# First block of a two-block model: attention's queries and keys ahead of the forget gates, and the gated recurrence in the last, skewed output projection

## The chip, the cores and the metric

The kernel runs on one core of one Trainium2 chip. The metric is the time of one launch in device microseconds (us). Before the change it is 1415.68 us, the median of three runs.

## What is computed

Two blocks of two layers each work on a sequence of 256 tokens of width 1024, in float32. The change touches the two layers of the first block. Each of them normalises the tokens, multiplies them with a wide input matrix, and runs three branches of width 512 on the columns of the product: causal attention with eight heads of 64 (queries and keys normalised by head and turned by a position-dependent rotation), a gated linear recurrence with four heads of 128 (HGRN), and attention over 256 rows of a memory with four heads of 128. Each branch is multiplied by silu of its own gate columns, and the three together by an output matrix:

```python
for l in range(DEPTH):
    h = rms_norm(x, norm_g[l])
    q_a, k_a, v_a, q_h, f_h, i_h, q_m, z = jnp.split(h @ w_in[l], split_points, axis=-1)
    o_a = moba_attention(qa, ka, va)                      # branch 0
    o_h = rms_norm(hgrn2_chunkwise(q_h, f_h, i_h, lb_all[l]), hgrn_o_norm[l])   # branch 1
    o_m = memory_attention(qm, km, vm)                    # branch 2
    y = jnp.concatenate([o_a, o_h, o_m], axis=-1) * jax.nn.silu(z)
    x = x + y @ w_out[l]
```

The second block (a delta rule, a retention and a pooling branch, then a gated feed-forward) follows and is not touched.

## The kernel before

The tokens lie in two tiles of 128 (t is 0 or 1). Every weight matrix is streamed once from memory in units of 256 rows x 512 columns. `Stream` keeps a list of the units in the order of their use (`units1` for this block, line 859 and on). A unit is loaded by SP into one of five `raw` buffers, ScalarE rounds it to a high half (`wh`), and VectorE makes the low half (`wl`, the difference), after which the raw buffer is free for the load five units later. A weight product is then three matmuls (high by high, high by low, low by high), which `mm3` issues at line 137; `aTh` and `aTl` are the two halves of the turned activations. Results lie in three PSUM banks named `acc` and five named `mx`.

`layer1` (line 920 and on) writes one layer. `tok` gives products with tokens as rows, `chan` with channels as rows (for `f_h` and `q_h` of the recurrence), `out_proj` the output projection. Everything that is not a weight product is a generator that is handed to `Order.spawn`. `Order` is a planner: it keeps modelled times of the engines, and after each group of three matmuls `poll` lets every waiting generator go one step whose inputs it believes to be ready. So weight products are the filler, and the branches' small steps stand between them in TensorE's order. A scheduler of the layer below may still shift instructions. The order of each engine is fixed when the program is built; a waiting instruction holds up all behind it on its engine.

Names that matter: `hgrn_f` makes the forget gates' sums `hA` and the gated keys `hk`; `hgrn` runs once for each of two pairs of heads, in eight levels of lengths 256, 128, ... 2 (`hgrn_z`: VectorE `hE`, ScalarE exponentials, VectorE `hZ`, then a product of `hZ` with itself on TensorE) and a last one of `hq` and `hk`; results of the five shortest levels are merged into `hST` by `COPY_PREDICATED` on VectorE. `hgrn_out` multiplies `hST` (and `hS01` of the earlier chunk) by `i_sb`, and normalises by head: a square (`junk`) on ScalarE, a sum (`ss`) on VectorE, logarithm and exponential on ScalarE (`y`), small steps, `on`. `gated` multiplies `on` by `sz`, turns the product `y` (transposes on TensorE) and splits it into `aTh` (ScalarE) and `aTl` (VectorE). `moba_in` and `moba` are the attention, `mem_attn` the attention over memory.

The order in a layer is: `i_h`, `v_a`, `f_h`, `q_h`, `q_a`, `k_a`, in layer 0 the memory's keys and values of both layers (16 units), `q_m`, and the gates `z` of branches 1, 0, 2. Then `out_proj` for branch 1 without skew, and once more for branches 0 and 2 with SKEW 4: all four units of a token tile run into one bank, first for t = 0 and then for t = 1, so that the next layer's norm of t = 0 starts while t = 1 is still being multiplied. Before each product `out_proj` joins the generators that make its operand.

## Time and profile before

| | us |
|---|---|
| median of three runs | 1415.68 |
| lowest and highest of them | 1414.83, 1417.45 |
| the profiled execution, its own time | 1415.08 |
| its span, first to last instruction | 1413.3 |
| TensorE matmul busy (7608 instructions) | 1386.1 |
| VectorE busy (1712 instructions) | 1017.3 |
| ScalarE busy (1420 instructions) | 829.5 |

The profile is one execution. Its trace has the start and the length of every instruction, and for the idle time ahead of one the engine or the transfer that ended it. PE is TensorE, DVE is VectorE, ACT is ScalarE, and SP issues the loads. Starts are in us from the beginning of the span. Matmuls overlap, so their spacing tells the pace and not their length. A float32 product that is no weight product leaves two records. Layer 0 of the first block ends at about 235 us, layer 1 at about 445.

### The profile page before, as it was taken

The numbers are of one execution on the slowest core, as the hardware profiler recorded it, in microseconds if no ns is written. First come the engines' busy times: TensorE is split into PE (matmuls) and PEld (weight loads), VectorE is DVE, ScalarE is ACT, GpSimd is POOL, SyncE is SP. The second block draws the span as 40 slices with busy tenths as digits, with TensorE's granted clock in tenths as the row PEclk, the third lists the DMA queues.
The fourth block names the chain that finished last, engine by engine and source line by source line (L and its number), as shares of the span: only waits on it lengthen the run. The fifth ranks groups of instructions, "written<-read, shape, count | busy, mean of one in ns | idle before, by whom it ended". The sixth has DMA issues, their size and how long they took to land.

```text
span 1413.3 us, 20451 instructions
## 1 busy us (share of the span) xinstructions
PE 1386.1 (98%) x7608; PEld 1166.4 (83%) x7608; DVE 1017.3 (72%) x1712; ACT 829.5 (59%) x1420; POOL 26.1 (2%) x65
## 2 busy tenths in 40 slices
PE   7999999999999999999999999999999999999998
PEld 6978887887888898888877888879888887788886
DVE  6798677689897698657777655687968567665564
ACT  6676565476764466556655544565666466555453
POOL 6100000000000000000000000000000000000000
PEclk9999999999999999999999999999999999999999
DMA  8653446555345454235665566645534357465561
GB/s 279 205 162 93 136 134 213 170 152 164 120 149 177 123 184 137 80 90 178 214 190 166 190 193 190 213 138 175 150 116 123 96 187 253 120 202 185 182 189 62
DMA packets 123412, 229.06 MB, mean 162 GB/s; under 512 B 10656, under 2 KB 16560, under 8 KB 123312
## 3 DMA queue, kind: packets, MB, share of 16 engines
q1 hardware_dynamic: 123280, 227.75, 51.7%
q8 instruction: 60, 0.98, 0.3%
q14 instruction: 40, 0.33, 0.1%
q0 software_dynamic: 32, 0.00, 0.0%
HBM read 226.67 MB, written 1.05 MB: 161 GB/s over the span
## 4 chain that ended last, share of the span: by engine, by line
PE 83%; DVE 6%; DMA 4%; ACT 3%; issue 3%; SPq 0%; DVEq 0%; ACTq 0%
PE acc L137 57%; PE mx L137 22%; PE mx L147 5%; DVE wl L109 2%; ACT wh L109 2%; DMA raw<-in_w_out 1%; DMA raw<-in_ffn_gate 1%; ACT junk L109 1%; DMA mem<-in_mem 0%; DVE hlf L109 0%; DMA gqk<-in_moba_q_norm 0%; DVE hA L109 0%; ACT sg L109 0%; DMA raw<-in_w_in 0%; SPq L408 0%
## 5 line engine op out<-in xcount | busy, mean ns | idle before, releaser
L109 DVE TENSOR_TENSOR wl<-raw,wh 128x1024 fp32r<-128x1024 f32 x396 | 479.9, 1221 | 148.4 <-ACT wh L109 142.9
L109 ACT CAST wh<-raw 128x1024 fp32r<-128x1024 f32 x396 | 412.7, 1050 | 173.6 <-PE acc L137 93.6
L137 PE MATMUL acc<-wh,aTh 128*128 128x512 f32 x1232 | 494.4, 402 | 2.4 <-ACT aTh L109 2.2
L137 PE MATMUL acc<-wh,aTl 128*128 128x512 f32 x1232 | 485.0, 394 | 1.1 <-DVE aTl L109 1.1
L137 PE MATMUL acc<-wl,aTh 128*128 128x512 f32 x1232 | 485.1, 394 | 0.0
L137 PEld LDWEIGHTS acc<-wh,aTl 128*128 128x128 f32 x1232 | 232.0, 188 | 49.8 <-DVE aTl L109 2.3
L137 PEld LDWEIGHTS acc<-wh,aTh 128*128 128x128 f32 x1232 | 232.3, 189 | 49.2 <-ACT aTh L109 4.1
L137 PEld LDWEIGHTS acc<-wl,aTh 128*128 128x128 f32 x1232 | 232.3, 189 | 45.0 <-issue 1.0
L137 PE MATMUL mx<-wh,ff 128*128 128x512 f32 x352 | 111.2, 392 | 0.0
L137 PE MATMUL acc<-aTh,wh 128*128 128x256 f32 x320 | 91.1, 285 | 0.0
L137 PE MATMUL acc<-aTh,wl 128*128 128x256 f32 x320 | 90.6, 283 | 0.0
L137 PE MATMUL acc<-aTl,wh 128*128 128x256 f32 x320 | 90.5, 283 | 0.0
L137 PEld LDWEIGHTS mx<-wh,ff 128*128 128x128 f32 x352 | 65.6, 188 | 13.2
L109 ACT ACTIVATE sg<-sg 128x512 f32<-128x512 f32 (+1 forms) x120 | 73.7, 614 | 1.5
L109 ACT ACTIVATE sg<-zc 128x512 f32<-128x512 f32 (+1 forms) x60 | 36.9, 616 | 62.4 <-DVE zc L109 62.3
L137 PE MATMUL mx<-wl,ff 128*128 128x512 f32 x176 | 68.5, 389 | 0.0
L137 PEld LDWEIGHTS acc<-aTh,wh 128*128 128x128 f32 x320 | 61.3, 192 | 0.3
L137 PEld LDWEIGHTS acc<-aTh,wl 128*128 128x128 f32 x320 | 61.3, 192 | 0.2
L137 PEld LDWEIGHTS acc<-aTl,wh 128*128 128x128 f32 x320 | 61.3, 192 | 0.0
L109 DVE TENSOR_SCALAR zc<-acc 128x512 f32<-128x512 f32 (+1 forms) x48 | 31.9, 664 | 36.8 <-PE acc L137 36.8
L109 ACT CAST ff<-mx 128x256 fp32r<-128x256 f32 x44 | 14.4, 375 | 52.8 <-PE mx L147 52.8
L109 ACT CAST aTh<-mx 128x512 fp32r<-128x512 f32 x44 | 24.7, 584 | 33.2 <-PE mx L147 32.9
(317 smaller groups left out, 1654.1 us busy)
## 6 DMA issues: line engine op xcount, KB each, us to landing
raw<-in_w_in SPq DMA_DIRECT2D x200, 512.0 KB
raw<-in_ffn_down SPq DMA_DIRECT2D x44, 512.0 KB
raw<-in_w_out SPq DMA_DIRECT2D x40, 512.0 KB
raw<-in_ffn_gate SPq DMA_DIRECT2D x40, 512.0 KB
raw<-in_ffn_up SPq DMA_DIRECT2D x40, 512.0 KB
raw<-in_w_mem_kv SPq DMA_DIRECT2D x16, 512.0 KB
raw<-in_w_branch_pool SPq DMA_DIRECT2D x8, 512.0 KB
raw<-in_w_branch_ret SPq DMA_DIRECT2D x8, 512.0 KB
```

Of the source, the lines that this page charges most:

```text
L109: r = f(out, *args, **kw)
L137: self._ns.matmul(out, lhsT, rhs, **kw)
L147: self._ns.transpose(out, x, ident)
```

## The change

Both layers of the first block are reordered. `q_a`, `k_a` and the attention come ahead of `f_h`, `q_h` and the recurrence; the gates are taken in the order 0, 1, 2; the first output projection, without skew, is that of branch 0, and the skewed one takes branches 1 and 2. The list of weight units is changed in the same way. No operation is added or removed.

```diff
@@ -877,15 +877,15 @@
             for br, k, i in self.proj_order(n, skew):
                 u.append((((l, "wo", br), (k, i)), rows(a["w_out"][l], 512 * br + 256 * k, 512 * i, 2, 512), skew > 0))
 
-        for n in ("i_h", "v_a", "f_h", "q_h", "q_a", "k_a"):
+        for n in ("i_h", "v_a", "q_a", "k_a", "f_h", "q_h"):
             cols(n, n in ("i_h", "v_a"))
         if l == 0:
             for m in range(self.depth1):
                 mem(m)
-        for n in ("q_m", "z1", "z0", "z2"):
+        for n in ("q_m", "z0", "z1", "z2"):
             cols(n)
-        wo((1,), 0)
-        wo((0, 2), SKEW)
+        wo((0,), 0)
+        wo((1, 2), SKEW)
         return u
 
     def proj_order(self, units, skew):
@@ -931,12 +931,6 @@
             o.spawn(self.constants(), "const")
             mem = self.new_hT()
             self.mem_norm(mem)
-        A, kx, qx = ([self.k2([P, 2, S], n) for _ in range(2)] for n in ("hA", "hk", "hq"))
-        st = {}
-        self.chan(hT, (l, "f_h"), lambda j, ps: self.hgrn_f(l, j, ps, A[j], kx[j]))
-        self.chan(hT, (l, "q_h"), lambda j, ps: self.chain(self.silu(qx[j], ps), self.hgrn(l, j, A[j], kx[j], qx[j], st)))
-        for t in range(NT):
-            o.spawn(self.hgrn_out(l, t, st, i_sb, on), f"on{l}1{t}")
         gqk = self.t(self.p_lay, [P, 2, 64], "gqk")
         for n, x in enumerate("qk"):
             self.load(gqk[:, n, :], a[f"moba_{x}_norm"][l].unsqueeze(0).to_broadcast([P, 64]))
@@ -949,22 +943,28 @@
         kT = [self.k2([P, 4, P], "kaT") for _ in range(NT)]
         for t in range(NT):
             o.spawn(self.moba(l, t, qk[t], ss[t], kT, v_sb, on), f"on{l}0{t}")
+        A, kx, qx = ([self.k2([P, 2, S], n) for _ in range(2)] for n in ("hA", "hk", "hq"))
+        st = {}
+        self.chan(hT, (l, "f_h"), lambda j, ps: self.hgrn_f(l, j, ps, A[j], kx[j]))
+        self.chan(hT, (l, "q_h"), lambda j, ps: self.chain(self.silu(qx[j], ps), self.hgrn(l, j, A[j], kx[j], qx[j], st)))
+        for t in range(NT):
+            o.spawn(self.hgrn_out(l, t, st, i_sb, on), f"on{l}1{t}")
         if not l:
             self.kv = [self.mem_kv(m, mem) for m in range(self.depth1)]
         kmT, vm = self.kv[l]
         self.tok(hT, [(l, "q_m")], lambda key, t, ps: self.mem_attn(l, t, ps, kmT, vm, on))
         ogain = self.ogain[l]
         oT = {}
-        for br in (1, 0, 2):
+        for br in (0, 1, 2):
             sz = [self.k2([P, G], "sz") for _ in range(NT)]
             self.tok(hT, [(l, f"z{br}")], lambda key, t, ps: self.silu(sz[t], ps))
             oT[br] = self.part()
             for t in range(NT):
                 o.spawn(self.gated(lambda key=(br, t): on[key], sz, oT[br], t, [f"on{l}{br}{t}"],
                                    ogain if br == 1 else None), f"oT{l}{br}{t}")
-        self.out_proj([(oT[1], (l, "wo", 1), [f"oT{l}1"])], 0, lambda t, ps: o.spawn(self.residual(t, ps)))
+        self.out_proj([(oT[0], (l, "wo", 0), [f"oT{l}0"])], 0, lambda t, ps: o.spawn(self.residual(t, ps)))
         nxt(None)
-        self.out_proj([(oT[br], (l, "wo", br), [f"oT{l}{br}"]) for br in (0, 2)], SKEW,
+        self.out_proj([(oT[br], (l, "wo", br), [f"oT{l}{br}"]) for br in (1, 2)], SKEW,
                       lambda t, ps: o.spawn(self.residual(t, ps, nxt(t)), f"h{self.ph + 1}{t}", True))
 
     def hgrn_f(self, l, j, ps, A, kx):
```

In layer 1, TensorE around the end of the recurrence, before: `mx_650` is the product of level 2 of the second pair of heads, `mx_651` the last level's, `mx_661` the result for t = 0, and `acc_659` are weight products of a gate.

```order
L137 MATMUL mx_650_4228<-hZ_645_4168 128x64 x4
L137 MATMUL mx_651_4236<-hq_478_3036,hk_476_3034 128x128 x4
L137 MATMUL acc_659_4268<-wl106_4177,aTh_429_2713 128x512
L137 MATMUL mx_661_4281<-i_sb_452_2839,hST_499_3339 128x128 x2
L137 MATMUL acc_659_4268<-wh106_4176,aTl_430_2714 128x512
L137 MATMUL acc_659_4268<-wh106_4176,aTh_429_2713 128x512
```

Weight products stood between the steps of the recurrence. Now, TensorE in the same layer from the last value product of the memory branch on (`mx_715` is level 2, `mx_717` the last level, `mx_718` the turned product of branch 2, `mx_719` and `mx_720` the recurrence's results for t = 0 and 1):

```order
L137 MATMUL mx_681_4387<-vm_260_1625,pT_709_4557 128x128 x4
L137 MATMUL mx_715_4587<-hZ_706_4522 128x64 x4
L137 MATMUL mx_717_4595<-hq_493_3208,hk_491_3206 128x128 x4
L147 MATMUL mx_718_4601<-ident_3_87,y_716_4592 128x128 x4
L137 MATMUL mx_719_4607<-i_sb_452_2839,hST_542_3620 128x128 x2
L137 MATMUL mx_720_4612<-i_sb_452_2839,hS01_543_3621 128x128
L137 MATMUL mx_720_4612<-i_sb_452_2839,hST_542_3620 128x128
```

The same steps follow each other with no weight product between them, behind the gates and behind the whole projection of branch 0. Eleven rows on in the same order (`mx_737` and `mx_738` turn the gated product of branch 1, `acc_713` is the first result of the skewed projection):

```order
L137 MATMUL mx_720_4612<-i_sb_452_2839,hST_557_3698 128x128
L137 MATMUL mx_720_4612<-i_sb_452_2839,hS01_558_3699 128x128
L137 MATMUL mx_720_4612<-i_sb_452_2839,hST_557_3698 128x128
L147 MATMUL mx_737_4658<-ident_3_87,y_735_4654 128x128 x4
L147 MATMUL mx_738_4663<-ident_3_87,y_736_4656 128x128 x4
L137 MATMUL acc_713_4577<-wh112_675_4354,aTh_654_4211 128x512
L137 MATMUL acc_713_4577<-wl112_676_4355,aTh_654_4211 128x512
L137 MATMUL acc_713_4577<-wh112_675_4354,aTl_655_4212 128x512
```

The skewed projection begins right behind the transposes of branch 1, and its first operand is `aTh_654`, what was turned there. Between `mx_704`, the product of level 4, and `mx_715` stand 14 weight matmuls, four transposes and four value products.

VectorE at the same place, from the result of level 4 to the operands of level 2 (`x0` is the residual sum):

```order
L109 COPY_PREDICATED hST_557_3698<-hgrn_masks_79_511,mx_704_4515 128x128x2
L109 TENSOR_TENSOR hE_705_4521<-hA_489_3204 128x512
L109 TENSOR_TENSOR wl116_4492<-raw116_4420,wh116_4491 128x1024
L109 TENSOR_TENSOR wl117_4528<-raw117_4433,wh117_4527 128x1024
L109 TENSOR_TENSOR x0_1_85<-acc_693_4430,x0_1_85 128x512
L109 TENSOR_TENSOR x0_1_85<-acc_694_4431,x0_1_85 128x512
L109 TENSOR_TENSOR hZ_706_4522<-hk_491_3206,hE_705_4521 128x256
L109 TENSOR_TENSOR hZ_706_4522<-hq_493_3208,hE_705_4521 128x256
```

Two halves of weights and two residual sums stand between the two steps of the recurrence. VectorE, further on, from the result of level 2 to the first small steps of the head norm:

```order
L109 COPY_PREDICATED hST_557_3698<-hgrn_masks_79_511,mx_715_4587 128x256
L109 TENSOR_TENSOR wl119_4679<-raw119_4489,wh119_4678 128x1024
L109 COPY_PREDICATED hST_557_3698<-hgrn_masks_79_511,mx_717_4595 128x512
L109 TENSOR_TENSOR aTl_692_4429<-mx_718_4601,aTh_691_4428 128x4x128
L109 TENSOR_TENSOR wl120_757_4756<-raw120_4513,wh120_756_4755 128x1024
L109 TENSOR_REDUCE ss_723_4626<-junk_721_4622 128x4
L109 TENSOR_REDUCE ss_724_4628<-junk_722_4624 128x4
L109 TENSOR_SCALAR v_725_4630<-ss_723_4626 128x4
L109 TENSOR_TENSOR w_727_4632<-y_726_4631 128x4
L109 SCALAR_TENSOR_TENSOR w_727_4632<-w_727_4632,v_725_4630 128x4
L109 SCALAR_TENSOR_TENSOR r_728_4633<-w_727_4632,y_726_4631 128x4
L109 TENSOR_SCALAR v_730_4642<-ss_724_4628 128x4
```

The steps of the norm stand behind `wl119`, `aTl_692` and `wl120`. ScalarE from the turned product of branch 2 to that of branch 1:

```order
L109 CAST aTh_691_4428<-mx_718_4601 128x4x128
L109 ACTIVATE junk_721_4622<-mx_719_4607 128x512
L109 ACTIVATE junk_722_4624<-mx_720_4612 128x512
L109 ACTIVATE y_726_4631<-ss_723_4626,eps0_6_95 128x4
L109 ACTIVATE y_726_4631<-y_726_4631 128x4
L109 ACTIVATE y_731_4643<-ss_724_4628,eps0_6_95 128x4
L109 ACTIVATE y_731_4643<-y_731_4643 128x4
L109 CAST wh125_762_4842<-raw125_4774 128x1024
L109 ACTIVATE aTh_654_4211<-mx_737_4658,cols_72_487 128x4x128
```

The rounding of a unit of the next stage, `wh125`, stands ahead of `aTh_654`.

## Rows read from the trace of the kernel before

**Rows 1.** The page: busy us of each engine; then engines' shares of the chain.

```profile
PE 1386.1 (98%) x7608; PEld 1166.4 (83%) x7608; DVE 1017.3 (72%) x1712; ACT 829.5 (59%) x1420; POOL 26.1 (2%) x65
...
PE 83%; DVE 6%; DMA 4%; ACT 3%; issue 3%; SPq 0%; DVEq 0%; ACTq 0%
```

**Rows 2.** Timeline, TensorE, layer 1: start us, us, engine, line, operation, tiles, shapes.

```profile
310.50 0.39 PE L137 MATMUL acc<-wl,aTh 128*128 128x512 f32 x1
310.73 0.39 PE L137 MATMUL acc<-wh,aTl 128*128 128x512 f32 x1
```

**Rows 3.** Busy us by engine in stretches of both layers; window, length, PE, PEld, DVE, ACT.

```profile
60.00:140.00 80.00, 79.36 (x544) 64.67 (x542) 72.50 (x159) 59.85 (x151) 0.00 (x0) 1.00 0.44 132
140.00:220.00 80.00, 79.38 (x428) 66.26 (x428) 57.36 (x102) 50.77 (x94) 0.00 (x0) 1.00 0.46 139
...
300.00:380.00 80.00, 78.95 (x526) 64.86 (x524) 73.39 (x144) 59.24 (x132) 0.00 (x0) 1.00 0.45 134
380.00:440.00 60.00, 58.69 (x345) 48.78 (x344) 46.67 (x83) 35.05 (x72) 0.00 (x0) 1.00 0.51 163
```

**Rows 4.** Timeline, TensorE, layer 1; in brackets the idle time ahead and its releaser.

```profile
313.07 0.71 PE L137 MATMUL mx<-hZ 128*128 128x128 f32 x4 [1.05 <-DVE hZ L109]
...
403.72 0.66 PE L147 MATMUL mx<-ident,y 128*128 128x128 f32 x4 [1.20 <-DVE y L109]
404.32 1.10 PE L137 MATMUL mx<-v_sb,pT 128*128 128x64 f32 x8
```

**Rows 5.** Timeline of SP, then TensorE, in layer 0; the last from the chain of waits.

```profile
37.21 0.46 SPq L408 DMA_DIRECT2D mem<-in_mem  x1
...
36.93 0.28 PE L137 MATMUL acc<-aTh,wh 128*128 128x256 f32 x1
...
53.10 4.53 DMA gqk<-in_moba_q_norm
```

**Rows 6.** Timeline of VectorE; then its groups from 262 to 440: count, busy, mean ns.

```profile
399.84 1.22 DVE L109 TENSOR_TENSOR wl<-raw,wh 128x1024 fp32r<-128x1024 f32 x1
400.98 0.15 DVE L109 SCALAR_TENSOR_TENSOR w<-w,v 128x4 f32<-128x4 f32 x1
...
402.38 0.69 DVE L109 TENSOR_TENSOR on<-mx,r 128x512 f32<-128x512 f32 x1
402.98 0.68 DVE L109 TENSOR_TENSOR y<-on,sz 128x512 f32<-128x512 f32 x1
...
L109 DVE TENSOR_TENSOR hE<-hA 128x512 f32<-128x512 f32 x12 | 8.2, 685 | 0.0
L109 DVE TENSOR_TENSOR hZ<-hk,hE 128x256 f32<-128x256 f32 x16 | 6.7, 421 | 1.0 <-ACT hE L109 1.0
...
L109 DVE COPY_PREDICATED hST<-hgrn_masks,mx 128x256 f32<-128x256 uint8 x8 | 4.7, 585 | 5.0 <-PE mx L137 5.0
...
L109 DVE SCALAR_TENSOR_TENSOR aTl<-mx,cols,aTh 128x512 fp32r<-128x512 f32 x2 | 1.5, 742 | 0.0
L109 DVE COPY_PREDICATED hST<-hgrn_masks,mx 128x512 f32<-128x512 uint8 x2 | 1.4, 721 | 0.0
```

**Rows 7.** Timeline of ScalarE near the end of layer 1.

```profile
394.17 0.31 ACT L109 ACTIVATE y<-ss,eps 128x4 f32<-128x4 f32 x1
394.51 0.21 ACT L109 ACTIVATE y<-y 128x4 f32<-128x4 f32 x1
396.35 1.05 ACT L109 CAST wh<-raw 128x1024 fp32r<-128x1024 f32 x1 [1.63 <-DMA raw<-in_w_out]
...
404.42 0.69 ACT L109 ACTIVATE aTh<-mx,cols 128x512 fp32r<-128x512 f32 x1 [0.17 <-PE mx L147]
```

**Rows 8.** The chain of waits near layer 1's end: start us, us, what.

```profile
391.85 4.48 DMA raw<-in_w_out
```

**Rows 9.** Timeline of TensorE at the start of the kernel.

```profile
13.43 0.63 PE L137 MATMUL acc<-wh,aTh 128*128 128x512 f32 x1
13.85 0.63 PE L137 MATMUL acc<-wl,aTh 128*128 128x512 f32 x1
```

## The prediction

> **What bounds the kernel now.** I read the page first. TensorE's matmuls fill 98% of the span, and 83% of the chain that ended last is TensorE [rows 1]; VectorE stands at 72% and ScalarE at 59%. A busy TensorE can still be a slow one, so I looked at its pace next: two weight products of 512 columns start 0.23 us apart (310.50, 310.73) wherever nothing is waited for [rows 2]. Then the stretches of the two layers that the change touches [rows 3]: TensorE idles 0.64 us of the 80 from 60, 0.62 of the next 80, 1.05 of the 80 from 300 and 1.31 of the 60 from 380, 3.6 us in all. Two gaps are most of the second layer's part: 1.05 us for the first operand of the recurrence and 1.20 us for a gated product [rows 4]. So the first block has almost nothing to win on TensorE: whatever the order, the same products have to run, and a reordering that filled every gap would give 3.6 us. What it can lose is open: TensorE takes its instructions in the order in which they stand, and a stretch with nothing but one dependent chain left in it costs the whole chain.
>
> **Part 1, the number of products, DMAs and vector operations.** The diff changes no operation, only their order, in both layers; each `wo` unit and each `z` unit is still loaded once. Price: 0.
>
> **Part 2, the beginning of layer 0.** The two `gqk` loads move on SP's queue from behind the mask loads to right behind the second `mem` load (37.21) [rows 5]; before, such a load took 4.53 us to land, so I expect it at about 42 to 43. VectorE now needs it to empty the first bank of `q_a`. There are three `acc` banks. The `q_a` products start at 36.93 [rows 5], and the fourth bank asked for (second half of `k_a`) is the first one again, 72 weight products and nine transposes later: 36.93 + 72 x 0.23 + about 0.9 = 54.4. On VectorE the emptying stands behind four halves of weights, the small `cols` operations and the two products of `mem`, which end at about 52.5 if the queue moves as it did before. The margin is some 1 to 2 us, so I take 0, and 2 us if that cover is gone. It is the only place in layer 0 that I found with a new short distance; its last part has the same shape as before, since the memory branch comes last in both.
>
> **Part 3, the end of layer 1.** Here the term is. Before, the recurrence ended at 389 to 393 with weight products standing between each of its steps, and two more branches came behind it; its gated product came as late as 403.72 [rows 4] and cost 1.20 us. Now the recurrence is the last thing to be ready, and the part that follows, `wo` of branches 1 and 2 with SKEW 4, begins with branch 1: TensorE stands in front of its first product until the whole tail of the recurrence is through. In the order of the changed program there is nothing between. I price the three holes that I see. VectorE operations of 512 elements start 0.60 us apart in a queue that never empties (402.38, 402.98), a half of weights takes 1.14 (399.84 to 400.98), and the others their mean less the same overlap of 0.08: 0.34 for `hZ`, 0.60 for `hE`, 0.51 and 0.64 for the two sizes of `hST` [rows 6].
>
> Hole 1, ahead of the operand product of level 2. VectorE, from the level 4 product's arrival: `hST` 0.51, `hE` 0.60, two halves of weights 2.28, two residual additions 1.20, two `hZ` 0.68: 5.3. ScalarE's two exponentials lie beside the weights. TensorE's own work meanwhile: 14 weight products 3.2, four transposes 0.6 (403.72 to 404.32 [rows 4]), four value products 0.92 (eight records that last 1.10, less the overlap of the last): 4.7. With some 0.2 us from a product's start to its reader, the hole is 0.8.
>
> Hole 2, ahead of the last state product. VectorE: reciprocal 0.1, addition 0.60, `on` 0.61, addition 0.60, weights 1.14, `y` 0.60, `hST` 0.51, weights 1.14, `hST` 0.64: 5.9. TensorE: the level products of 2 and 1, 1.8; transposes 0.6; seven products of the finished state at 0.23, 1.6: 4.0. Hole 1.9, and 0.2 for the way between engines: 2.1.
>
> Hole 3, from the last `hST` to the first products of `wo`. VectorE first clears `aTl` 0.60 and a half of weights 1.14. Then nothing is queued but the chain: reduction 0.68; on ScalarE logarithm and exponential 0.55 (from 394.17 to 0.21 after 394.51) [rows 7]; three small steps 0.5; `on` 0.60; three small steps of the other half 0.45 (its operations alternate with these on VectorE); its `on` 0.60; `y` 0.68; four transposes 0.66 [rows 4]; `aTh` on ScalarE 0.69 [rows 7]; `aTl` 0.74 [rows 6]. That is 7.9 us to the third product of `wo`, in which TensorE has 2.8 of its own (five state products 1.1, eight transposes 1.2, two products 0.45). Hole 5.1. One thing more stands in it: on ScalarE the cast `wh125` (1.05 [rows 7]) is queued ahead of `aTh`, and its load can start only once VectorE has finished `wl120`, 1.74 us into the hole. A load of that size landed 4.48 us after its issue in this stretch [rows 8], so the cast ends 7.3 us in, where `aTh` could start at 6.5: 0.8 at that row, 0 if the load takes 0.8 less; I take 0.6, near the row.
>
> Together 0.8 + 2.1 + 5.1 + 0.6 = 8.6 us of new waiting. Off it go the two old gaps [rows 4], since the first operand of the recurrence now has the value products of the attention and some 18 us of TensorE in front of it, and the old gated wait is gone: 1.05 + 1.20 = 2.25. Net +6.35. The profiled run took 1415.08 us, 1.8 more than its span of 1413.3, which gives 1421.4; the median of the runs lies 0.6 above that run, so against it the sum is 1422.0.
>
> **The clock.** At the beginning of this trace, after an idle start, weight products start 0.43 us apart (13.43, 13.85) [rows 9], against 0.23 later [rows 2]: 1.2 and 2.4 GHz. The column of the granted clock reads full even there, so I go by spacing. Thirteen products at the slow pace cost 13 x 0.2 = 2.6 us. Nowhere later in the trace is there a gap of more than 1.3 us in these layers, and none slowed anything. In the new tail TensorE stands still for about 4 us in one piece, and then turns the two tiles and stands again for over 1 us. The Trainium skill ("TensorE: Matmul & The Clock Gate", section What's actually happening) says that the slow level is the default and that an idle array falls back to it; by that rule the tail is paid twice. The start of this trace agrees with the first half; no row shows the second, a fall from full speed.
>
> **The rivals.**
> The clock falls: the mechanism above, with its hole, and the first 13 or more products of `wo` at half pace. 1422 + 2.6 = 1425, up to 1428 if all of the first half's 24 to 30 go slowly. For it: a longer standstill than any that this trace has once it runs. Against it: transposes lie in it.
> The chain is mostly hidden: VectorE is ahead of where I put it, because the recurrence began earlier relative to TensorE than the queue suggests. Then holes 1 and 2 close, hole 3 loses its 1.74 of older work in part and keeps about 4.4, and against the old 2.25 and some of layer 0's 1.2 us of idle it leaves +1.5: 1417.
> Faster than before, the other side: with the attention first, VectorE, which was busy 73.4 of the 80 us from 300 [rows 3], is relieved where the recurrence loads it most, every old gap closes, and the last level's `hST` ends before TensorE has run out of its own work. The price is then the 3.6 us of idle: 1412. The point from which this decides is the 8.6 us above: the recurrence must end that much earlier than its place in VectorE's queue says, or TensorE must have some 37 more weight products beside it. The program's order shows neither.
> That the change only trades an early wait for a late one (part 2's bank wait of 2 us on top of the sum) is inside the range.
>
> **How the numbers follow.** Forecast 1422, chance 0.52, with its own range of 1419 to 1424.5. Clock falls 0.28, 1425. Hidden 0.14, 1417. Faster 0.06, 1412. A measurement of this kernel tells about 0.2% (2.8 us) from no change, so the first two cases count as slower (0.80), the third as the same (0.14), the last as faster (0.06). The range of 8 in 10 takes in the forecast, most of the hidden case and the clock's upper part: 1417 to 1427.
>
> **What would show it.** Right: in the profile after, TensorE idle ahead of the transposes of a gated `y` of about 4 to 5 us in one wait near 430, VectorE as its releaser, ahead of the last `acc` and `mx` products of layer 1, and 8 to 10 us of idle in that layer's last 40 us; the gap before the first `hZ` of layer 1 gone; layers of the second block unchanged in length. The clock rival shows as products 0.43 apart right behind it. Wrong: less than 4 us of idle there, or new idle of over 2 us before 220 us (the bank of `q_a`, a late operand of the attention), which would put the loss in layer 0.

## The result and the profile after

The changed kernel takes 1423.13 us in the median (1422.34 to 1424.71), against 1415.68 before: a ratio of 1.0057, with a 95% interval of 1.0045 to 1.0068. The forecast was 1422.0 with a range of 1417 to 1427. In a later set of runs the ratio was 1.0045 (1.0029 to 1.0062).

The page of the profiled execution shows almost nothing of the loss. TensorE's busy time is the same to 0.3 us and has the same number of products (the first line of [rows 1] is its counterpart); only the span has grown, by 7.9 us. The operations are the same in number, but four copies have moved from ScalarE (1420 to 1416) to VectorE (1712 to 1716), the engine that turns out to be late.

```profile
span 1421.2 us, 20465 instructions
...
PE 1386.4 (98%) x7608; PEld 1168.0 (82%) x7608; DVE 1020.1 (72%) x1716; ACT 829.2 (58%) x1416; POOL 26.2 (2%) x65
```

The stretches that stand in [rows 3] for the kernel before tell more. The columns are the window, its length, and then the busy us of PE, PEld (TensorE's weight loads), DVE, ACT and POOL, each with its number of instructions; the last three are the granted clock of TensorE as a share of full speed, the busy share of the DMA engines and GB/s.

```profile
60.00:140.00 80.00, 78.86 (x587) 67.81 (x586) 67.02 (x145) 58.42 (x150) 0.00 (x0) 1.00 0.43 130
140.00:220.00 80.00, 77.79 (x454) 65.19 (x453) 62.25 (x115) 49.26 (x92) 0.00 (x0) 1.00 0.45 139
300.00:380.00 80.00, 79.75 (x598) 69.51 (x597) 70.84 (x136) 61.69 (x138) 0.00 (x0) 1.00 0.46 137
380.00:440.00 60.00, 52.95 (x333) 45.12 (x332) 50.57 (x90) 33.54 (x64) 0.00 (x0) 0.94 0.49 159
426.00:431.00 5.00, 0.52 (x5) 0.33 (x3) 4.73 (x14) 2.45 (x7) 0.00 (x0) 0.80 0.90 295
431.00:436.00 5.00, 4.66 (x15) 3.73 (x16) 2.30 (x4) 2.06 (x3) 0.00 (x0) 0.52 0.49 199
```

TensorE's idle time (window less PE busy) in the first four windows is 1.14, 2.21, 0.25 and 7.05 us, where it was 0.64, 0.62, 1.05 and 1.31. So 5.7 us of new idle lie at the end of layer 1, 1.6 in the second half of layer 0 and 0.5 in its first half, and 0.8 came back in the third window, where the recurrence's first operand had been late. The last two rows show the core of it: between 426 and 431 TensorE works for half a microsecond while VectorE is busy for 4.73 of the 5, and right behind that TensorE's granted clock is 0.52 in the mean, next to the lower of its two levels (1.2 of 2.4 GHz).

TensorE's timeline in that place, with the idle time ahead of an instruction and its releaser in brackets:

```profile
417.68 1.16 PE L137 MATMUL mx<-vm,pT 128*128 128x128 f32 x8 [0.21 <-ACT pT L109]
419.22 1.10 PE L137 MATMUL mx<-hZ 128*128 128x64 f32 x8 [0.38 <-DVE hZ L109]
...
422.81 0.66 PE L147 MATMUL mx<-ident,y 128*128 128x128 f32 x4 [1.54 <-DVE y L109]
...
426.13 0.39 PE L137 MATMUL mx<-i_sb,hST 128*128 128x128 f32 x2
431.34 1.94 PE L147 MATMUL mx<-ident,y 128*128 128x128 f32 x8 [4.82 <-DVE y L109]
433.20 0.80 PE L137 MATMUL acc<-wh,aTh 128*128 128x512 f32 x1
433.80 0.63 PE L137 MATMUL acc<-wl,aTh 128*128 128x512 f32 x1
434.22 0.63 PE L137 MATMUL acc<-wh,aTl 128*128 128x512 f32 x1
...
435.50 0.56 PE L137 MATMUL acc<-wh,aTl 128*128 128x512 f32 x1
435.89 0.40 PE L137 MATMUL acc<-wh,aTh 128*128 128x512 f32 x1
436.13 0.39 PE L137 MATMUL acc<-wl,aTh 128*128 128x512 f32 x1
```

These are the three holes of the prediction: 0.21 + 0.38, then 1.54, then 4.82 us. (The expectations below put them at about 0.9, 2.0 and 5.0: they count from start to start at the usual pace, the brackets from the modelled end of the product ahead.) Behind the last one the eight transposes take 1.94 us (four take 0.66 at 422.81), and the weight products start 0.43 us apart until 435.50, then 0.23 again. What VectorE and ScalarE did in the meantime:

```profile
424.97 0.68 DVE L109 TENSOR_TENSOR aTl<-mx,aTh 128x512 fp32r<-128x512 f32 x1
425.56 1.22 DVE L109 TENSOR_TENSOR wl<-raw,wh 128x1024 fp32r<-128x1024 f32 x1
426.70 1.28 DVE L109 TENSOR_REDUCE ss<-junk 128x4 f32<-128x512 f32 x2
...
428.64 0.69 DVE L109 TENSOR_TENSOR on<-mx,r 128x512 f32<-128x512 f32 x1
...
429.90 0.69 DVE L109 TENSOR_TENSOR on<-mx,r 128x512 f32<-128x512 f32 x1
430.51 1.28 DVE L109 TENSOR_TENSOR y<-on,sz 128x512 f32<-128x512 f32 x2
...
430.63 1.04 ACT L109 CAST wh<-raw 128x1024 fp32r<-128x1024 f32 x1 [2.09 <-DMA raw<-in_w_in]
432.46 0.69 ACT L109 ACTIVATE aTh<-mx,cols 128x512 fp32r<-128x512 f32 x1 [0.78 <-PE mx L147]
```

VectorE is never idle for long up to 431.8: the low half of an older operand (`aTl`) and an older half of weights first, then the normalisation of the two tiles, then the two gated products that TensorE waits for. The last line matters for one term of the sum: `aTh` waits for the transposes (0.78 <-PE), not for the cast ahead of it, which has ended at 431.67.

The second block runs the same instructions in the same order in both kernels, and yet takes 774.2 us before and 775.2 after in these two traces. The table below shows that this is scatter between executions.

### The profile page after: what moved, and what is told of

Read it like the earlier page. It is cut to its first block, busy times and chain, and to the rows that moved or that the text cites. A ratio compares the mean times of both kernels' runs of the same rounds, so it can differ in the third digit from the quotient of the medians.

```text
span 1421.2 us, 20465 instructions
## 1 busy us (share of the span) xinstructions
PE 1386.4 (98%) x7608; PEld 1168.0 (82%) x7608; DVE 1020.1 (72%) x1716; ACT 829.2 (58%) x1416; POOL 26.2 (2%) x65
## 3 DMA queue, kind: packets, MB, share of 16 engines
HBM read 226.67 MB, written 1.05 MB: 160 GB/s over the span
## 4 chain that ended last, share of the span: by engine, by line
PE 83%; DVE 6%; ACT 4%; issue 3%; DMA 3%; SPq 0%; DVEq 0%; ACTq 0%
PE acc L137 58%; PE mx L137 22%; PE mx L147 4%; DVE wl L109 2%; ACT wh L109 1%; DMA raw<-in_w_out 1%; DMA raw<-in_ffn_gate 1%; ACT junk L109 1%; ACT he L109 0%; ACT aTh L109 0%; ACT sg L109 0%; DVE x L109 0%; DMA baw<-in_w_in 0%; DVE hlf L109 0%; DVE hA L109 0%
## 5 line engine op out<-in xcount | busy, mean ns | idle before, releaser
L109 DVE TENSOR_TENSOR wl<-raw,wh 128x1024 fp32r<-128x1024 f32 x396 | 479.8, 1221 | 146.3 <-ACT wh L109 140.8
L109 ACT CAST wh<-raw 128x1024 fp32r<-128x1024 f32 x396 | 412.2, 1050 | 166.5 <-PE acc L137 92.9
L137 PE MATMUL acc<-wh,aTh 128*128 128x512 f32 x1232 | 494.6, 402 | 2.9 <-ACT aTh L109 2.8
L137 PE MATMUL acc<-wh,aTl 128*128 128x512 f32 x1232 | 484.9, 394 | 1.2 <-DVE aTl L109 1.2
L137 PE MATMUL acc<-wl,aTh 128*128 128x512 f32 x1232 | 484.9, 394 | 0.0
L137 PEld LDWEIGHTS acc<-wh,aTh 128*128 128x128 f32 x1232 | 232.5, 189 | 50.6 <-ACT aTh L109 5.1
L137 PEld LDWEIGHTS acc<-wh,aTl 128*128 128x128 f32 x1232 | 232.2, 188 | 50.4 <-DVE aTl L109 2.8
L137 PEld LDWEIGHTS acc<-wl,aTh 128*128 128x128 f32 x1232 | 232.6, 189 | 44.7 <-issue 1.0
L137 PE MATMUL mx<-wh,ff 128*128 128x512 f32 x352 | 111.2, 392 | 0.0
L137 PE MATMUL acc<-aTh,wh 128*128 128x256 f32 x320 | 91.7, 286 | 0.0
L137 PE MATMUL acc<-aTl,wh 128*128 128x256 f32 x320 | 90.8, 284 | 0.0
L137 PE MATMUL acc<-aTh,wl 128*128 128x256 f32 x320 | 90.6, 283 | 0.0
L137 PEld LDWEIGHTS mx<-wh,ff 128*128 128x128 f32 x352 | 65.6, 188 | 13.2
L109 ACT ACTIVATE sg<-sg 128x512 f32<-128x512 f32 (+1 forms) x120 | 73.8, 615 | 1.7
L109 ACT ACTIVATE sg<-zc 128x512 f32<-128x512 f32 (+1 forms) x60 | 37.0, 616 | 59.1 <-DVE zc L109 58.9
L137 PE MATMUL mx<-wl,ff 128*128 128x512 f32 x176 | 68.5, 389 | 0.0
L137 PEld LDWEIGHTS acc<-aTh,wh 128*128 128x128 f32 x320 | 61.3, 192 | 0.4
L137 PEld LDWEIGHTS acc<-aTh,wl 128*128 128x128 f32 x320 | 61.3, 192 | 0.2
L137 PEld LDWEIGHTS acc<-aTl,wh 128*128 128x128 f32 x320 | 61.3, 192 | 0.1
L109 DVE TENSOR_SCALAR zc<-acc 128x512 f32<-128x512 f32 (+1 forms) x48 | 31.9, 665 | 36.6 <-PE acc L137 36.6
L109 ACT CAST aTh<-mx 128x512 fp32r<-128x512 f32 x44 | 24.8, 588 | 35.9 <-PE mx L147 35.8
L109 ACT CAST ff<-mx 128x256 fp32r<-128x256 f32 x44 | 14.4, 376 | 52.8 <-PE mx L147 52.8
```

The lines of the kernel that those rows point to most:

```text
L109: r = f(out, *args, **kw)
L137: self._ns.matmul(out, lhsT, rhs, **kw)
```

## The experiments

Most kernels here are the changed one with the choices of the change made separately for each layer. The edit is the same in all of them, and each is then given by its four tables (entry 0 is layer 0):

```diff
-        for n in ("i_h", "v_a", "q_a", "k_a", "f_h", "q_h"):
+        for n in ("i_h", "v_a") + (("q_a", "k_a", "f_h", "q_h") if LATE[l] else ("f_h", "q_h", "q_a", "k_a")):
-        for n in ("q_m", "z0", "z1", "z2"):
+        for n in ("q_m",) + tuple(f"z{br}" for br in Z_ORDER[l]):
-        wo((0,), 0)
-        wo((1, 2), SKEW)
+        wo(FIRST[l], 0)
+        wo(REST[l], SKEW)
```

`layer1` follows the same tables. The four added lines move the line numbers in these traces by four: L113, L141 and L151 are the helpers L109, L137 and L147. Three sections of each trace are compared, cut where the second tile's normalised input is first turned: from layer 0's to layer 1's, from there to the second block's, and through the second block to the start of its last feed-forward part. A ratio is always against runs of the kernel before in the same set.

| kernel | layer 0 | layer 1 | second block | ratio | 95% interval |
|---|---|---|---|---|---|
| before | 245.3 | 195.5 | 774.2 | 1 | |
| changed | 246.9 | 200.8 | 775.2 | 1.0057 | 1.0045 to 1.0068 |
| `after_again` | 246.3 | 200.9 | 776.8 | 1.0045 | 1.0029 to 1.0062 |
| `l1_only` | 244.4 | 201.2 | 774.4 | 1.0045 | 1.0031 to 1.0059 |
| `l0_only` | 249.2 | 194.5 | 774.2 | 1.0027 | 1.0015 to 1.0038 |
| `warm18` | 245.9 | 198.8 | 774.5 | 1.0044 | 1.0031 to 1.0057 |
| `swap_last` | 246.7 | 197.6 | 775.2 | 1.0032 | 1.0019 to 1.0045 |
| `no_norm` | 246.3 | 198.2 | 775.7 | 1.0038 | 1.0025 to 1.0051 |
| `order_only` | 246.4 | 207.9 | 774.5 | 1.0098 | 1.0083 to 1.0113 |
| `zwo_only` | 244.2 | 194.0 | 774.4 | 0.9986 | 0.9977 to 0.9994 |
| `zwo_again` | 244.8 | 193.9 | 774.9 | 0.9982 | 0.9973 to 0.9990 |
| `zwo_both` | 245.1 | 193.5 | 774.2 | 0.9983 | 0.9974 to 0.9992 |
| `ord0` | 246.4 | 193.8 | 775.4 | 0.9991 | 0.9982 to 0.9999 |

Layer 0's column needs care. The section begins at 15 to 17 us, where TensorE's clock has risen in some traces and not in others: the eight transposes there take 0.84 + 1.27 us in the kernel before, 0.82 + 0.71 in the changed one and 0.49 + 0.71 in `l1_only`. Counted instead from the 61st product into an `acc` bank (27 to 29 us) to the same end, layer 0 takes 232.1 us before, 234.5 in the changed kernel and 236.0 in `l0_only`.

### Which layer loses

`l1_only`, the change in layer 1 alone:

```diff
+LATE = (0, 1)
+Z_ORDER = ((1, 0, 2), (0, 1, 2))
+FIRST = ((1,), (0,))
+REST = ((0, 2), (1, 2))
```

> Layer 0 keeps the order of the kernel before, layer 1 has the changed one. The trace of the changed kernel puts the start of layer 1's second normalisation 1.4 us later than before, the end of layer 1 another 5.3, the rest of the program 1.0. Theory (the loss is the tail of the recurrence at the end of layer 1, which TensorE waits out): 1415.7 + 5.3 = 1421.0, with the waits of about 0.9, 2.0 and 5.0 us unchanged near 417 to 432. Rival (the two layers work together, the shift of layer 0 makes part of it): 1419 or less, with a smaller wait. If the 1.0 us of the second block belongs to layer 1's order, 1422.

Layer 1 took 201.2 us with waits of the same sizes, layer 0 took 244.4, in the range of its old order, and the whole was 1.0045 times the kernel before, +6.4 us (4.4 to 8.3). The loss of layer 1 needs nothing from layer 0.

`l0_only`, the change in layer 0 alone:

```diff
+LATE = (1, 0)
+Z_ORDER = ((0, 1, 2), (1, 0, 2))
+FIRST = ((0,), (1,))
+REST = ((1, 2), (0, 2))
```

> Layer 0 has the changed order, layer 1 keeps the one of before. Theory: layer 0 costs the 1.4 us that the two traces show, nearly all of it in one wait of 2.1 us near 216 us, where ScalarE waits for a weight half and a gate stands behind its cast: 1417.1, and the wait is there again. Rival (that wait is an accident of one execution, and the early bank wait that I had allowed up to 2 us for is nil): 1415.7, no wait over 1 us near 216.

It lost 3.8 us (2.1 to 5.4), more than the 1.4 expected. The wait near 216 is there again (1.29 to 2.13 us in the seven traces with layer 0 as changed), and this time TensorE's clock fell behind it, which it had not done at the same place in the changed kernel. TensorE's timeline, and two windows as above:

```profile
219.57 0.78 PE L151 MATMUL mx<-ident,y 128*128 128x128 f32 x4 [2.13 <-DVE y L113]
220.01 0.77 PE L141 MATMUL acc<-wh,aTl 128*128 128x512 f32 x1
220.58 0.63 PE L141 MATMUL acc<-wh,aTh 128*128 128x512 f32 x1
...
216.00:220.00 4.00, 1.87 (x11) 1.32 (x10) 3.37 (x6) 2.88 (x5) 0.00 (x0) 0.99 0.46 139
220.00:224.00 4.00, 4.00 (x13) 3.18 (x12) 2.73 (x4) 3.30 (x5) 0.00 (x0) 0.59 0.38 120
```

By the later count of layer 0 the 3.8 us is the sum of two things: 2.0 us that the change costs there (the mean of the six traces whose clock held against that of the six with the recurrence first), and 1.8 more here, where the clock fell.

What TensorE waits for there is seen in the changed kernel's trace. ScalarE first, then VectorE, then TensorE:

```profile
213.12 1.05 ACT L109 CAST wh<-raw 128x1024 fp32r<-128x1024 f32 x1 [4.74 <-DMA raw<-in_w_out]
214.07 0.63 ACT L109 ACTIVATE sg<-zc 128x512 f32<-128x512 f32 x1
214.73 1.30 ACT L109 ACTIVATE sg<-sg 128x512 f32<-128x512 f32 x2
...
217.34 0.68 DVE L109 TENSOR_TENSOR y<-on,sz 128x512 f32<-128x512 f32 x1
...
218.16 0.63 PE L147 MATMUL mx<-ident,y 128*128 128x128 f32 x4 [2.12 <-DVE y L109]
```

ScalarE stands for 4.74 us in front of the cast of a weight load that has not landed, and the three passes of a gate are queued behind that cast. The gated product comes as late as the gate. Before, the same cast started at the same time, but only one pass of the gate stood behind it:

```profile
213.21 1.05 ACT L109 CAST wh<-raw 128x1024 fp32r<-128x1024 f32 x1 [1.37 <-DMA raw<-in_w_out]
217.97 0.66 PE L147 MATMUL mx<-ident,y 128*128 128x128 f32 x4 [0.60 <-DVE y L109]
```

### Is layer 0's wait the place of one turn?

Two kernels, both with the gates and projections of layer 1 in the new order and the recurrence first there. `zwo_both` has only the gates' order new in layer 0, `ord0` only the order of the work. First `zwo_both`:

```diff
+LATE = (0, 0)
+Z_ORDER = ((0, 1, 2), (0, 1, 2))
+FIRST = ((0,), (0,))
+REST = ((1, 2), (1, 2))
```

> Only the order of the gates and output projections is the new one, in both layers; the recurrence stays ahead of the attention in both. In layer 0 the loss of the changed kernel sits in one wait near 216 (2.1 us against 0.6 before): the gated product of the second branch's second tile, whose gate stands on ScalarE behind the cast of a late weight half, with 12 weight products of TensorE between its turn and that of the tile before it (19 in the kernel before). Theory (the wait comes of that place in the order, which needs both parts of the change): here 19 products lie between again, the wait is 0.6, and the kernel takes what the one with the new gate order in layer 1 alone takes, 2 us less than before. Rival (the order of the gates alone makes the loss of layer 0): wait of 2 us, 0 to 1 us over before.

Then `ord0`:

```diff
+LATE = (1, 0)
+Z_ORDER = ((1, 0, 2), (0, 1, 2))
+FIRST = ((1,), (0,))
+REST = ((0, 2), (1, 2))
```

> Layer 0 with the attention ahead of the recurrence but with the gates and projections in the order of before (branch 1 first); layer 1 with the new order of gates and projections alone. 21 weight products lie between the two turns here. Theory (the place of the turn in TensorE's order decides): wait near 216 of 0.7 us or less, 2 us less than before in all. Rival (the new order of work in layer 0 costs by itself, by its own short waits near 70, 81 and 93 or by the load): 0 to 2 us over before.

`zwo_both` keeps layer 0 at 245.1 us: the gates' order costs nothing there by itself. `ord0` has the single wait of 2.1 us split in two of about half a microsecond:

```profile
PE mx L151 <- DVE y L113: 1.1, 2, 0.5
```

(line of the waits of TensorE from 140 to 262: us in total, times, longest), but its layer 0 still takes 246.4 us. So the theory that the place of that one turn makes the loss fell. The six traces with the changed layer 0 whose clock held there have 245.9 to 246.9 us, `ord0` 246.4, and the six with the recurrence first in layer 0 (the sixth is `fill_021`, below) have 244.2 to 245.3: the order of the work costs some 1.7 us. By the later count, which leaves the rise of the clock out, it is 233.8 us for `ord0`, 233.7 to 234.6 for the six and 231.9 to 232.5 with the recurrence first: 1.7 us for the order of the work, 2.0 for the whole change. Of that the trace of `ord0` shows 0.40 and 0.60 in front of the attention's first turns and 1.1 for the two gated products, while 0.6 of the kind stood at 216 before and another wait of the beginning is gone. Which of these small pieces belongs to which cause stays open.

### The last wait is a chain, not a weight load

`no_norm` takes the normalisation out of the recurrence's output in layer 1:

```diff
-        r = yield from self.rms_heads(ps)
+        if l == 0:
+            r = yield from self.rms_heads(ps)
         o = self.k2([P, 4, P], "on")
-        self.dve.tensor_tensor(o, ps, self.bc(r), op=ALU.mult)
+        if l == 0:
+            self.dve.tensor_tensor(o, ps, self.bc(r), op=ALU.mult)
+        else:
+            self.dve.tensor_copy(o, ps)
```

> The changed kernel without the normalisation of the recurrence's output in layer 1 (square, reduction, logarithm, exponential and the small steps are left out, the product with the factor is a copy): the chain behind the last state product is some 2.7 us shorter (in the trace of the changed kernel from 426.7, where VectorE is through with older work, to 428.5 instead of 431.2). Theory (the last wait is that chain): the wait of 5.0 us shrinks to about 2.3. If the clock then holds, the slow products go as well: 7.4 us over before becomes 7.4 - 2.7 - 1.7 = 3.0; if it still falls, 4.7. Rival (the wait hangs on the weight loads and the halves made of them, not on the chain): the wait stays near 5, 7.4 over before.

TensorE's timeline:

```profile
428.74 1.23 PE L147 MATMUL mx<-ident,y 128*128 128x128 f32 x8 [2.54 <-DVE y L109]
430.14 0.80 PE L137 MATMUL acc<-wh,aTh 128*128 128x512 f32 x1 [0.17 <-ACT aTh L109]
430.73 0.63 PE L137 MATMUL acc<-wl,aTh 128*128 128x512 f32 x1
...
433.29 0.43 PE L137 MATMUL acc<-wh,aTl 128*128 128x512 f32 x1
433.57 0.40 PE L137 MATMUL acc<-wh,aTh 128*128 128x512 f32 x1
```

The wait fell from 4.82 to 2.54 us, by 2.3 where the theory had 2.7; a wait set by the weights would have stayed. Layer 1 took 198.2 us, 2.8 less than the 201.0 that the three traces of the changed order have in the mean. The clock fell all the same, after a wait about half as long: the products are 0.43 us apart up to 433.29. The whole was +5.4 us (3.5 to 7.2), next to the 4.7 expected for a clock that still falls.

### The clock

`warm18` gives TensorE something to do in that wait:

```diff
         yield needs
+        if needs == ["on110"]:
+            warm = self.mx()
+            for _ in range(18):
+                self.pe.matmul(warm, self.ident_bf, self.ident_bf.unsqueeze(1).to_broadcast([P, 4, P]), start=True, stop=True)
```

> The changed kernel with 18 more products of 512 columns (bf16, into a bank that nothing reads) put in front of the transposes of the gated recurrence in layer 1, so that TensorE is busy for about 4 of the 5 us that it waits there. Theory (behind the wait eight transposes and six products run at half pace because the clock fell while TensorE stood still, 1.7 us on the path): products 0.23 apart right behind the transposes, 1423.1 - 1.7 = 1421.4. Rival (the slow products wait for something else, or the added products hold up the chain): still 0.43 apart, 1423.1, or 1424 if they are in the way.

```profile
424.87 3.83 PE L137 MATMUL mx<-ident_bf 128*128 128x512 bf16 x17
428.72 0.63 PE L147 MATMUL mx<-ident,y 128*128 128x128 f32 x4
430.51 0.63 PE L147 MATMUL mx<-ident,y 128*128 128x128 f32 x4 [1.16 <-DVE y L109]
430.99 0.50 PE L137 MATMUL acc<-wh,aTh 128*128 128x512 f32 x1
431.32 0.39 PE L137 MATMUL acc<-wl,aTh 128*128 128x512 f32 x1
431.55 0.40 PE L137 MATMUL acc<-wh,aTh 128*128 128x512 f32 x1
```

Four transposes take 0.63 us again, the weight products start 0.23 us apart from the second on, and the granted clock is 1.00 from 424 to 433. Layer 1 took 198.8 us, 2.0 to 2.4 less than in the three traces of the changed order (200.8 to 201.2), and that is what the fallen clock costs there, or a little more: with 18 more products in the planner's order one gated product on VectorE also comes earlier (at 427.88, not behind both normalisations). The rival, slow products that wait for something else, is out. The time of the whole kernel does not show the gain: 1.0044 (1.0031 to 1.0057) overlaps with both measurements of the changed kernel, 1.0057 and 1.0045, so it rests on layer 1's section.

### More of TensorE's own work beside the chain

`swap_last` takes branch 2 ahead of branch 1 in layer 1's skewed part:

```diff
+LATE = (1, 1)
+Z_ORDER = ((0, 1, 2), (0, 1, 2))
+FIRST = ((0,), (0,))
+REST = ((1, 2), (2, 1))
```

> The changed kernel, but in layer 1 the skewed part takes branch 2 ahead of branch 1: 24 products of branch 2 can now stand between the last steps of the recurrence, 24 x 0.2275 = 5.5 us of work. Theory (the chain on VectorE and ScalarE sets the end, TensorE has too little beside it): the first two waits close (2.9 us) and the last shrinks by the three products left there (0.7), so some 4 us: 1419 (1417.5 to 1420.5). Rival (VectorE's whole queue is late, so that more products of TensorE only pull more halves of weights ahead of the chain): the last wait grows by what the first two lose, 1422 to 1423.

The first two holes close. Of the last, 4.05 us stay, and the clock falls (TensorE's timeline):

```profile
428.20 0.40 PE L141 MATMUL acc<-wh,aTl 128*128 128x512 f32 x1
432.64 1.94 PE L151 MATMUL mx<-ident,y 128*128 128x128 f32 x8 [4.05 <-DVE y L113]
```

Layer 1 took 197.6 us, 3.4 less than in the changed order, and the whole was +4.5 us (2.7 to 6.4) against the 7.4 of the changed kernel: 2.9 less where the theory had 4 (1.9 against the 6.4 of `after_again`), more than the rival's 0 to 1.

`fill_021` goes further. The last part is branches 2 and 1 with a skew of 2, so that all 48 products of branch 2 come first, 27 of them behind the recurrence's last state product:

```diff
+LATE = (0, 1)
+Z_ORDER = ((1, 0, 2), (0, 2, 1))
+FIRST = ((1,), (0,))
+REST = ((0, 2), (2, 1))
-        wo((1, 2), SKEW)
+        wo(REST[l], SKEW if l == 0 else 2)
```

> Layer 0 as before; layer 1 with the attention first, as in the changed kernel, but the gates in the order 0, 2, 1 and the last part as branches 2 and 1 with a skew of 2: all 48 products of branch 2 for both tiles come ahead of the first of branch 1, 27 of them behind the last state product of the recurrence (27 x 0.2275 = 6.1 us, the wait there was 5.0). Theory (the loss is TensorE with nothing to do beside that chain, and the clock that falls over it): all three waits close and the clock holds; layer 1, 195.1 us in the kernel before and 200.4 to 200.8 in the changed order, loses 7.9 of waits and 1.7 of slow products: 191 to 193, and the whole 2 to 4 us less than before. Rival (VectorE's queue is the bound, and filling TensorE only moves the wait): 195 or more, the same as before or slower.

```profile
433.47 1.23 PE L151 MATMUL mx<-ident,y 128*128 128x128 f32 x8 [0.98 <-DVE y L113]
448.14 1.29 PE L151 MATMUL mx<-ident,xn 128*128 128x128 f32 x8 [2.06 <-DVE xn L113]
...
425.00:440.00 15.00, 13.85 (x68) 11.09 (x68) 11.14 (x21) 6.14 (x12) 0.00 (x0) 1.00 0.80 265
```

The long wait is down to 0.98 us and the clock holds (1.00 in the window from 425 to 440). But the kernel is not faster than before: 1.0007 (0.9998 to 1.0015). With a skew of 2 fewer products are left to stand behind the first tile's residual, so TensorE now waits 2.06 us for the next layer's normalised input. (For that reason its sections can't be cut as in the table.) From the first turn of layer 1's input to that of the feed-forward part in the second block's first layer it takes 486.4 us, the kernel before 486.2 and `l1_only` 492.2. (The 195.1 and 200.4 to 200.8 of the expectation are layer 1 between the first turns of its two ends.) Against `l1_only` 9.6 us were to go and 5.8 went: 0.98 us of the old wait stayed, 2.06 came back at the next norm, and 0.8 is left over, which may be no more than the counting: the 9.6 takes the old waits as 7.9, the brackets say 6.95. Closing the waits of TensorE only moved the last of them, as the rival said, though by another way than VectorE's queue alone.

### Which part of the change costs

`order_only` has layer 0 as changed, layer 1's work in the new order and its gates and projections in the old one; `zwo_only` the reverse, with layer 0 as before. First `order_only`:

```diff
+LATE = (1, 1)
+Z_ORDER = ((0, 1, 2), (1, 0, 2))
+FIRST = ((0,), (1,))
+REST = ((1, 2), (0, 2))
```

> Layer 0 as in the changed kernel; in layer 1 only the order of the branches' work is the new one (attention ahead of the recurrence), while the gates and the first output projection keep branch 1 first, as before. The 48 products of branch 0's projection (10.9 us) now stand behind the recurrence's end and not beside it. Theory (the path is the recurrence's chain with VectorE's and ScalarE's whole queue, of which the four weight units of that projection are 4 x 2.28 = 9.1 us of VectorE's): the chain ends earlier by part of the 9.1 us and TensorE has 10.9 us less beside it, so 1 to 6 us more than the changed kernel, 11 over before (8 to 14). Rival (the chain does not move when weight halves go): 18 over before. Other rival (the new order of gates and projections is itself what costs): 3 over before or less.

Then `zwo_only`:

```diff
+LATE = (0, 0)
+Z_ORDER = ((1, 0, 2), (0, 1, 2))
+FIRST = ((1,), (0,))
+REST = ((0, 2), (1, 2))
```

> Layer 0 as before; in layer 1 only the order of the gates and of the output projections is the new one (branch 0 first, branches 1 and 2 in the skewed part), while the recurrence keeps its place ahead of the attention. The recurrence then ends with weight products beside it, so the three waits at layer 1's end should not be there; what can be late is the attention, whose gated product already cost 1.2 us before and now has 48 products less ahead of it. Theory: layer 1 within 0 to 4 us of before, 2 over it as my value, with a wait for the attention's y of 2 to 5 us, and none of 5 us for the recurrence's. Rival (the order of gates and projections is the cause of the loss): 5 us or more over before with the long wait for y of branch 1.

`order_only` is the slowest of all, +13.9 us (11.7 to 16.0), inside the range of its theory, though 6.5 over the changed kernel where the theory had 1 to 6. It has more waits than one, and the last of them is as long as in the changed kernel (TensorE's timeline):

```profile
404.32 2.08 PE L141 MATMUL mx<-vm,pT 128*128 128x128 f32 x8 [2.01 <-DVE pT L113]
410.66 1.24 PE L151 MATMUL mx<-ident,pexp 128*128 128x128 f32 x4 [1.40 <-ACT pexp L113]
...
426.36 1.94 PE L151 MATMUL mx<-ident,y 128*128 128x128 f32 x8 [4.96 <-DVE y L113]
```

Waits are only part of it, and its theory had no clock: the four value products behind the first of these waits take 2.08 us (1.16 in the changed kernel, at 417.68), the eight transposes behind the last 1.94, and the granted clock is 0.73 from 405 to 410, 0.62 from 410 to 415 and 0.54 from 427 to 432. From 235 to 470 TensorE idles 7.1 us more than before (9.4 against 2.4), while layer 1 is 12.9 longer than the 195.0 of its old order; the slow products would account for the rest, though no run takes the two apart.

`zwo_only` is faster than the kernel before. The wait for a gated product at 403.72 [rows 4] is gone, and TensorE is busy for 59.91 of the 60 us from 380 (58.69 in [rows 3]):

```profile
380.00:440.00 60.00, 59.91 (x352) 49.88 (x351) 48.38 (x87) 36.00 (x76) 0.00 (x0) 1.00 0.51 162
```

I had expected a later attention to cost 2 us; no wait for its product is left in that stretch. The same kernel was run again, beside the changed kernel on one chip:

> The kernel with the new order of gates and projections in layer 1 alone once more, beside the changed kernel on the same chip. Theory: it stays 2.0 us (0.8 to 3.3) under before, TensorE idle for less than 0.5 us of layer 1's last 60. Rival (the gain was an accident of its runs): the same as before within 0.5 us.

It was 0.9982 (0.9973 to 0.9990), 2.5 us under before, with TensorE busy for 59.93 of the 60 us from 380. So the half of the change that reorders the gates and projections is a gain of 2.0 to 2.5 us, of which layer 1's section shows 1.2 (means of four traces and of two); where the rest lies is open. The half that puts the attention first is the whole loss in layer 1, and there the gates' new order rescues part of it: +13.9 becomes +7.4. So the two halves do not add up; the new order of the gates is worth more where the recurrence comes last. The kernels with the gates' order alone beat both the kernel before and the changed one.

And the changed kernel itself once more:

> The changed kernel once more, to have it on the same chip as the others. Theory: 7.4 us over before (6 to 9.6), the three waits at layer 1's end within 0.1 us of 0.9, 2.0 and 5.0 and slow products behind the last; the second block the same length as before within 1 us, since its order of work is the same (the 1.0 us that it was longer in the first trace is scatter between executions). Rival (the second block is really longer by 1.0): again 775.2 against 774.2.

It had the same waits in layer 1 (0.21, 0.37, 1.54 and 4.82) and the fallen clock again, at +6.4 us (4.1 to 8.8). Its second block took 776.8 us, and the thirteen traces of the table, which all run the same order there, 774.2 to 776.8. The 1.0 us of the first trace is no effect of the change. Part of the scatter is the clock: in `after_again` its granted share is 0.52 from 937.0 to 940.5 in the second block, and in `swap_last` 0.51 from 933.3 to 936.7.

## Why the prediction was right, and where it was not

**The number of operations.** Right: 7608 products in both, and the second block the same within its scatter. That four copies would move to VectorE was not foreseen, and no run prices it.

**Layer 0.** The step that failed. The short distance that I had priced at 0 to 2 us, the bank that `q_a` has to give back, costs nothing: TensorE does not wait once between 20 and 70 us. But I wrote that the last part has the same shape as before and looked no further, and layer 0 costs 2.0 us (1.4 in the sections of this pair of traces, where the slow start of the trace before hides part). The prediction's sign for a loss in layer 0, over 2 us of new idle before 220 us, is just met (0.50 + 1.59), though most of the loss lies in layer 1. The last part has the same shape by branches; the place of a gate behind a late cast on ScalarE is another, and so are the attention's first waits.

**The end of layer 1.** Right in mechanism, and nearly so in place and size. Hole 1 was put at 0.8 and measured 0.59, hole 2 at 2.1 and 1.54 (and 0.11 more between the state products), hole 3 at 5.1 and 4.82; the idle time there came to some 7 us, under the 8 to 10 given as a sign. Hole 2 stood earlier than written, ahead of the transposes of branch 2, whose `y` is the sixth step of that sum. Hole 3's 5.1 was some 4.7 ahead of the transposes and 0.4 behind them; the first measured 4.82, the second did not come, as the transposes ran slowly. VectorE's queue was the reason in all three (but for 0.21 of hole 1, which ScalarE's `pT` ended): from the level 4 `hST` at 413.78 to the end of the second `hZ` at 419.16 it took 5.4 us where the sum had 5.3. What had to be read for this was the order of VectorE's queue with the weight halves in it, not only the recurrence's own operations. The cast `wh125`, 0.6 in the sum, cost 0: `aTh` waited for TensorE's transposes.

**The old gaps.** Both went, as said. In all, layer 1 is 5.3 us longer in the first pair of traces; the mean of the three changed layers 1 (201.0) less that of the two old ones with nothing else changed (195.0) is 6.0, against 6.35 in the sum, which has no slow clock in it.

**The clock.** Wrong side chosen. The forecast held that the clock stays up; its rival, 0.28, was what happened, in every trace that has a wait of 2.5 us or more there. The start of the trace before [rows 9] had shown the slow pace but no fall. Now the rows from 431 do: granted clock 0.52, products 0.43 us apart. The rule of the Trainium skill that I had weighed ("TensorE: Matmul & The Clock Gate", section What's actually happening: the slow level is the default and an idle array falls back to it) agrees with these rows, where the array stood still for 4.82 us; falls behind much shorter waits are at the end of this document. The price of the fall was smaller than my 2.6 us and fell elsewhere too: five intervals at 0.43 instead of 0.23 are 1.0 us and eight transposes another 0.8, together 1.8, and `warm18` put it at 2.0 to 2.4, with one gated product that also came earlier.

**Why the total came out.** That 1422.0 lies so near 1423.1 is in good part luck. The clock (some 2 us) and layer 0 (2.0) were missing; the cast (0.6) and about 1 us of the holes went the other way, and so did something in layer 1 that I can't place: 6.95 us of waits and 1.8 of slow products, less the 2.25 of old gaps, are 6.5, where layer 1 grew by 5.3 in this pair and 6.0 in the mean. Two traces of one kernel also differ by 1 to 2 us outside the changed part.

**The other rivals.** Faster and hidden are out by the three waits. The point that I gave for the first, some 37 more weight products beside the recurrence, was nearly tried: `fill_021` had 48 of branch 2 there, closed the waits but for 0.98 us, and came back to the time of the kernel before, not below it.

## What to carry to other kernels

Before moving a long dependent chain to the end, count what the in-order engine still has to do beside it and set that against the helper engine's whole queue, older work included; here three sums of VectorE's queue gave the waits to within 0.6 us. A reorder has parts that can be timed one by one: in layer 1 one half of this one is a gain of 2 us and the other, alone, a loss of over 10. Each wait of 2.5 to 5 us on TensorE here cost more than itself, since products behind it ran at half pace; a wait that work closes can still reappear at the next place that this work used to cover.

## What was not expected of the hardware

The clock does not follow the length of a wait alone. Behind 2.12 us at 218 in the changed kernel the granted clock stayed at full and products started 0.23 us apart; behind 2.13 us at the same place in `l0_only` it was 0.59 from 220 to 224. After 2.54 us in `no_norm` the eight transposes ran in 1.23 us and only the products behind them were slow; after 4.82 and 4.05 us the transposes were slow too (1.94 us). Five slow intervals between weight products followed in the changed kernel, eight in `swap_last`. In `order_only` it fell behind 2.01 us and again, 6.3 us later, behind 1.40. And in the second block of `after_again` weight products were 0.43 us apart from 938.59 to 939.87 behind two waits of only 0.77 and 0.71 us (at 934.56 and 936.50), while the changed kernel kept full pace behind 0.78 and 0.64 at the same place.
